# A decoder block on one Trainium2 core: larger portions for the attention, seven products for the first half of a gating projection, and a later read of the residual

## The chip, the cores and the metric

The kernel runs on one core of one Trainium2 chip. The metric is the device time of one execution in microseconds; lower is better. Three executions before the change took 1574.31, 1574.32 and 1574.69 us, a median of 1574.32. A further execution was recorded by the hardware profiler, and all durations and positions in this text come from it.

Engine names in the profile: PE is TensorE (matmuls), PEld its weight loads, DVE is VectorE, ACT is ScalarE, POOL is GpSimd, SP is the engine whose queue issues most DMAs. L12 is line 12 of the kernel before.

## The reference

One layer of a decoder trunk: 256 positions, 2048 channels, everything in float32. Three token mixers share one input projection, a gate per channel weighs each of them, and a feed-forward part follows.

```python
h = rms_norm(x, norm_mix_pre)
proj = h @ w_in                       # a_in, b_in, q, kv, nsa_g, merge_g
y_a = conformer_conv(a_in, ...)       # GLU, causal depthwise convolution of 31, LayerNorm, swish, @ w_a_out
y_b = chunked_spatial_gating(b_in, ...)                                   # ..., @ w_b_out
y_c = native_sparse_attention(q, kv, nsa_g, ...)   # compressed, selected and window attention, @ w_c_out
g_a, g_b, g_c = split(sigmoid(merge_g), 3)
mixed = (g_a * y_a + g_b * y_b + g_c * y_c) @ w_o
x = x + rms_norm(mixed, norm_mix_post)
h = rms_norm(x, norm_ffn_pre)
u_g, u_v = split(causal_dwconv3(h @ w_up), 2)
x = x + rms_norm((silu(u_g) * u_v) @ w_down, norm_ffn_post)
```

merge_g has 3 x 2048 columns: 2048 gates for each of the branches A (convolution), B (spatial gating) and C (attention).

## The kernel before

**Exact float32 from fp32r.** TensorE multiplies in a format called fp32r. Every operand is therefore split into a high part (the value rounded to fp32r, by ScalarE) and a low part (the remainder, by VectorE), and a product is three matmuls: high x high, high x low, low x high. `mm_t` (L195 to L198) issues such a triple; its three lines are the ones the profile shows for the projections with tokens on the partitions.

**Weights.** All weights stream from memory once. `fetch` (L104) reads 128 x 1024 float32 (512 KB) through SP's queue into one of five buffers `wraw`. `piece` (L132) and `weights` (L906) split it into `whi` and `wlo`, which have four buffers each; these eight buffers are a ring used in program order by everything that streams weights, and `ring` (L913) takes them for the sevens too. `granule` (L151) is two pieces, 24 matmuls in a gating projection.

**Scratch.** Three rings of large on-chip buffers matter here: `s16` with three buffers (xt, cv, At, Bt, Ct, ep, mh, ml, x2 in their turn) and one more outside P1 (mac, then y1, sf, back), `s8` with four, and `q1` with twelve buffers of 128 x 256. PSUM has four banks with the tag acc for the projections and four for everything else; `banks(2, 1)` recasts the second four as two single banks and one double one while the attention runs, and `banks(4, 0)` turns them back.

**Order of stages.** RMSNorm and the input projections come first, up to about 303 us in the profile. Then come the gated branches, `branch(bi, act_of)` (L994). Branch 0 is B, with its activations in Bt; branch 1 is A, with At; branch 2 is C, with Ct. For every column block of 512 output channels a branch runs the gating projection (four quarters of 24 matmuls, tiles pg, from hT), takes tanh of the gates (mg), runs the branch's own output projection (two halves of 24, tiles py), and adds the gated product into `mac`. Branches 0 and 1 have four column blocks. Branch 2 has two; the other half of its columns is done by seven products (below). After that come w_o (its first 1024 columns by seven products), the up-projection with the short convolution, and the down-projection in two halves of columns, `Pair(0)` and `Pair(1)`.

**Portions of background work.** Much of the work of the three mixers doesn't stream weights: the depthwise convolution (`conv_gen`), the layer norm of branch A with its activations At (`lna_gen`, L483), the compressed keys and values (`cmp_prep`, `cmp_gen`, L593 and L610), the scores of the compressed part (`cmp_attn`), and the attention itself (`attn`, L856). Each is a Python generator that issues a few instructions and yields a cost in nominal nanoseconds. The generators wait in a queue `bg`, and the projections call `pump` (L92) between their weight tiles:

```python
    def pump(ns):
        debt[0] = min(debt[0], 0.0) + ns if not bg else debt[0] + ns
        while bg and debt[0] > 0:
            try:
                debt[0] -= next(bg[0])
            except StopIteration:
                bg.popleft()
```

Each call adds one portion of `ns` units to an account and issues background work until the account is used up. The portion has a size for every stage; for the branches it is `BG`. In a branch one portion is issued after each 24 matmuls. `until(name)` (L200) issues all background work up to a mark, without an account: branch 0 needs "B" (Bt complete), branch 1 "A" (At), branch 2 "C" (the attention, Ct). `cmp_gen` streams weights too: its w1 pieces come through `piece`, in the same `wraw`, `whi` and `wlo` buffers, and its matmuls (zp) multiply them with bk, which `cmp_prep` writes. Program order sets who gets a buffer and which instruction has priority where several are ready; splits in `piece` are raised in priority by `PR`, 1000 places, and the framework orders each engine's instructions by these priorities and its own simulated times. Where the text speaks of `fixed` (L889) or `in_line` (L190), the order on an engine is written out by hand instead.

**Seven products.** `in_sevens` (L970) computes two column blocks at once, 2 x 128 tokens by 2 x 512 columns. For three pairs of k-tiles (`NG` = 3) it uses a scheme of seven block products where eight are usual: sums and differences of weight blocks, made by VectorE (`Seven.seven`, L940), meet sums and differences of activations (`sums4`, L837). Such a pair costs 21 matmuls in place of 24. The ten other k-tiles go the usual way. A `Seven` needs four banks for the results and four for side products, so all of the PSUM. The sums of hT for the gating projections are made in the background (`input_sums`, tile sh); those of the mixed activations, for w_o, are made after the gating stage by `sums4` into tiles `sm` (L1104 to L1107). `mix_gen` (L1047) transposes finished column blocks of mac into mh and ml.

**The residual.** The input of the last residual addition, y1, is written to memory (`spill`, L1345) and read back into `back` during the second half of the down-projection. That half runs through ten quads (`second.quad(j)`, one pair of k-tiles by seven products each) with plain k-tiles in between, and keeps six plain tiles (`kept`) for the end. After the loop, SP's queue gets a row of gains (L1508), `second.combine()` gathers the side products, and the six kept tiles finish the four results one after another, followed by the norm, the residual addition (`fin`, L1532) and the stores.

Of the kernel before, what the change touches and what calls it, by code (L numbers as in the profile page):

```python
# [30 lines left out]
D = 2048  # L32
T = 256
# [9 lines left out]
BA, BB, BC, BG = 2100, 2200, 2200, 2500  # L43
# [14 lines left out]
def block(ctx: ExitStack, tc: tile.TileContext, x, xf, fp, cst, rows, sgw, w1, w2, wf_a, wt_bv, wf_bu, wf_c,  # L58
# [935 lines left out]
    def branch(bi, act_of):  # L994

        for cb in range(2 if bi == 2 else 4):
# [46 lines left out]
            if bi == 2:  # L1043
                bg.append(mix_gen(cb))
            pump(BUDGET)

    def mix_gen(cb):  # L1047

        for j in range(2 * cb, 2 * cb + 2):
# [10 lines left out]
            if j < NG:  # L1060
# [8 lines left out]
    branch(2, lambda: Ct_box["t"])  # L1069
    mh, ml = mix["h"], mix["l"]  # L1070


    gates = s8([128, 2, 2, 512], F32, "gates")
    tt = s8([128, 2048], F32, "tt")
    pr = Seven([PS.tile([128, 512], F32, tag="acc", name=f"pga{i}") for i in range(4)],
               [bank([128, 512], f"pgb{i}") for i in range(4)])
    pr.at = lambda t, n: gates[:, t, n]
# [11 lines left out]
    def wp(n, k):  # L1089
        return weights(wt_p[20 + 2 * n + k // 4][:, k % 4 * 512:k % 4 * 512 + 1024])  # L1090

    pump(1e6)
# [4 lines left out]
    for n in range(2):  # L1097
        for t in range(2):
            fixed(V, V.tensor_add, gates[:, t, n], pr.c[t][n], gates[:, t, n])
            fixed(S, S.activation, gates[:, t, n], gates[:, t, n], AF.Tanh, scale=rh[:, t:t + 1])  # L1100
        if n == 0:
            early.append(wp(0, 4))
    with tc.issue_after(seq[V][0]):
        for j in range(NG):  # L1104
            if j % 2 == 0:
                mix[j // 2] = s8([128, 2, 2, 4, 128], R, f"sm{j}")
            sums4(*mix["a", j], mix[j // 2][:, j % 2], f"m{j}")  # L1107
    pump(1e6)
    Ct = Ct_box["t"]
    for n in range(2):  # L1110
        cb = 2 + n
        py = [bank([128, 512], f"pyc{t}") if n == 0 else PS.tile([128, 512], F32, tag="acc", name=f"pyd{t}")
              for t in range(2)]
        for k in range(8):
            if k % 2 == 0:
                hi, lo = early.pop(0) if early else wp(n, k)
# [540 lines left out]
```

## Time and profile before

| what | value |
|---|---|
| median of three executions | 1574.32 us |
| the profiled execution, its own time | 1575.5 us |
| its span on the core | 1573.8 us |
| TensorE busy | 1561.2 us, 99% of the span |
| VectorE busy | 1274.0 us, 81% |
| ScalarE busy | 906.6 us, 58% |
| DMA, mean over the span | 194 GB/s read and written |

The stages by the profile's clock: input projections and the layer norm's inputs to 303 us, branch 0 to 443, branch 1 to 608, the two column blocks of branch 2 to 688, the seven-product stage of its other half to 731 and its products to 753, w_o to 842, the up-projection to 1335, the down-projection's first half to 1448 and its second to 1564.6; the rest of the 1573.8 is the last norm, addition and store.

How to read it: all positions are microseconds from the start of the span. A row of a timeline has the start, the busy time, the engine, the line, the operation and its output and input tiles, a count where several equal ones are put together, and in brackets the engine's idle time before it and what ended that. A row of busy times by stretch has the stretch, its length, and then for each engine the busy time and the count of instructions in brackets, the granted TensorE clock (1.00 is full speed), the DMA engines' mean busy share and GB/s. TensorE's matmuls are pipelined: the listed duration of a 128x512 matmul is 0.39 us, but in a steady stream one begins every 0.227 us.

### The profile page before, as it was taken

The page shows a single profiled execution, that of the slowest core. Times are in us where ns is not written, and L with a number is a line of the kernel's source. Part 1 is how long each engine was busy: PE and PEld are TensorE (multiplying, and loading weights), DVE is VectorE, ACT ScalarE, POOL GpSimd, SP SyncE. Part 2 cuts the span into 40 slices and gives each one's busy share as a digit, 9 for nine tenths or more (in the row PEclk, how much of TensorE's full clock was granted, in tenths as well). Part 3 has the DMA queues.
Part 4 walks back from the last instruction along what each step waited for, and adds up shares of the span by engine and source line. Part 5 has one row for each costly group of instructions (what it writes and reads, how often), then busy time and mean ns, then how long its engine had stood idle before and what let it go on. Part 6 is the DMA issues. An engine that isn't in the chain of part 4 may idle for free.

```text
span 1573.8 us, 22431 instructions
## 1 busy us (share of the span) xinstructions
PE 1561.2 (99%) x8155; PEld 1324.4 (84%) x8155; DVE 1274.0 (81%) x2192; ACT 906.6 (58%) x1462; POOL 17.7 (1%) x46
## 2 busy tenths in 40 slices
PE   9999999999999999999999999999999999999997
PEld 7888889888888787788888888888888888888876
DVE  7799999858866655479878988888777777899898
ACT  7544544447646775656566655555555555556563
POOL 1000020000000000000000000000000000000000
PEclk9999999999999999999999999999999999999999
DMA  9565556665765445456784666666666666766672
GB/s 376 181 193 180 190 178 206 197 196 179 235 200 160 155 140 173 135 164 211 251 271 162 200 188 189 189 191 192 189 188 192 187 195 189 227 208 207 201 269 93
DMA packets 85440, 307.95 MB, mean 196 GB/s; under 512 B 9808, under 2 KB 10832, under 8 KB 84304
## 3 DMA queue, kind: packets, MB, share of 16 engines
q1 hardware_dynamic: 83952, 301.91, 60.1%
q0 software_dynamic: 944, 4.19, 0.7%
q8 instruction: 64, 1.05, 0.3%
q10 hardware_dynamic: 432, 0.41, 0.1%
q14 instruction: 48, 0.39, 0.1%
HBM read 301.23 MB, written 4.19 MB: 194 GB/s over the span
## 4 chain that ended last, share of the span: by engine, by line
PE 96%; DVE 2%; DMA 1%; ACT 0%; issue 0%; DVEq 0%; SPq 0%; ACTq 0%
PE ps L176 29%; PE ps L183 15%; PE pd0b L930 5%; PE pg L197 5%; PE pg L198 5%; PE pg L196 5%; PE pd1a L930 4%; PE py L197 2%; PE py L198 2%; PE py L196 2%; PE poa L930 2%; PE pga L930 2%; PE pd0a L930 2%; PE po L198 1%; PE po L196 1%; PE po L197 1%
## 5 line engine op out<-in xcount | busy, mean ns | idle before, releaser
L148 DVE TENSOR_TENSOR wlo<-wraw,whi 128x1024 fp32r<-128x1024 f32 x400 | 486.3, 1218 | 117.0 <-ACT whi L147 110.0
L147 ACT ACTIVATE whi<-wraw 128x1024 fp32r<-128x1024 f32 x400 | 418.8, 1052 | 186.7 <-PE pg L198 79.4
L176 PE MATMUL ps<-h2T,whi 128*128 128x512 f32 x1360 | 325.0, 391 | 0.0
L176 PEld LDWEIGHTS ps<-h2T,whi 128*128 128x128 f32 x1360 | 249.8, 188 | 48.2
L183 PEld LDWEIGHTS ps<-h2T,wlo 128*128 128x128 f32 x1360 | 174.5, 191 | 6.7
L183 PE MATMUL ps<-h2T,wlo 128*128 128x256 f32 x1360 | 176.6, 283 | 0.0
L176 PE MATMUL ps<-hT,whi 128*128 128x512 f32 x640 | 157.4, 392 | 0.0
L218 ACT ACTIVATE t<-ps 128x256 f32<-128x256 f32 x125 | 47.6, 382 | 187.1 <-PE ps L176 186.7
L176 PEld LDWEIGHTS ps<-hT,whi 128*128 128x128 f32 x640 | 116.0, 189 | 21.2
L198 PE MATMUL pg<-whi,hT 128*128 128x512 f32 x320 | 125.9, 393 | 0.0
L197 PE MATMUL pg<-wlo,hT 128*128 128x512 f32 x320 | 125.8, 393 | 0.0
L196 PE MATMUL pg<-whi,hT 128*128 128x512 f32 x320 | 122.2, 393 | 0.0
L895 DVE TENSOR_TENSOR wlowraw<-wraw,whiwraw 128x1024 fp32r<-128x1024 f32 x72 | 87.0, 1222 | 28.3 <-ACT whiwraw L895 27.1
L219 DVE TENSOR_TENSOR t<-ps,t 128x256 f32<-128x256 f32 x125 | 52.5, 421 | 70.4 <-ACT t L218 70.0
L479 DVE SCALAR_TENSOR_TENSOR cv<-hb,fps,cv 128x256 f32<-128x256 f32 x240 | 104.8, 476 | 0.2 <-ACT cv L475 0.2
L895 ACT ACTIVATE whiwraw<-wraw 128x1024 fp32r<-128x1024 f32 x72 | 75.3, 1058 | 33.6 <-PE pd0b L930 8.0
L183 PEld LDWEIGHTS ps<-hT,wlo 128*128 128x128 f32 x640 | 84.6, 190 | 4.7
L183 PE MATMUL ps<-hT,wlo 128*128 128x256 f32 x640 | 86.8, 283 | 0.0
L197 PEld LDWEIGHTS pg<-wlo,hT 128*128 128x128 f32 x320 | 60.1, 188 | 13.8 <-issue 1.1
L198 PEld LDWEIGHTS pg<-whi,hT 128*128 128x128 f32 x320 | 60.1, 188 | 12.7 <-issue 0.7
L196 PEld LDWEIGHTS pg<-whi,hT 128*128 128x128 f32 x320 | 59.8, 188 | 12.3 <-issue 0.3
L1385 ACT ACTIVATE fa<-fs,fps 128x256 f32<-128x256 f32 x88 | 52.4, 595 | 1.1 <-DVE fs L221 0.9
(1258 smaller groups left out, 2652.1 us busy)
## 6 DMA issues: line engine op xcount, KB each, us to landing
wraw<-in_wf_up_dram SPq DMA_DIRECT2D x176, 512.0 KB, 4.3
wraw<-in_wt_g_dram SPq DMA_DIRECT2D x80, 512.0 KB, 3.8
wraw<-in_wt_p_dram SPq DMA_DIRECT2D x48, 512.0 KB, 4.0
wraw<-in_wt_dn_dram SPq DMA_DIRECT2D x48, 512.0 KB, 4.4
wraw<-in_wf_a_dram SPq DMA_DIRECT2D x32, 512.0 KB, 4.5
wraw<-in_wt_dq_dram SPq DMA_DIRECT2D x20, 512.0 KB, 4.8
qa<-in_wt_dq_dram SPq DMA_DIRECT2D x20, 512.0 KB, 4.2
wraw<-in_wf_bu_dram SPq DMA_DIRECT2D x16, 512.0 KB, 4.2
```

The costliest lines, as they stand in the source:

```text
L147: S.activation(hi[:, :n], raw[:, :n], AF.Copy)
L148: V.tensor_sub(lo[:, :n], raw[:, :n], hi[:, :n].bitcast(F32))
L176: ins = PE.matmul(ps[:, :, ts], lhsT=ws[k // 8][0][:, c:c + 128], rhs=mov[:, k, :, ts], start=(k == 0 and not t), stop=(k == n - 1), skip_ ...
L183: ins = PE.matmul(ps[:, 1, ts], lhsT=ws[k // 8][1][:, c:c + 128], rhs=mov[:, k, 0, ts], start=False, stop=False, skip_group_check=True).ins
L196: PE.matmul(ps, lhsT=xh, rhs=hi, start=first, stop=False)
L197: PE.matmul(ps, lhsT=xh, rhs=lo, start=False, stop=False)
L198: return PE.matmul(ps, lhsT=xl, rhs=hi, start=False, stop=last).ins
L219: V.tensor_add(t1 if rb is not None else dst, ps[:, 0], t1)
L479: V.scalar_tensor_tensor(ca[:, j], hb[:, j, k:k + T], w(j, k), ca[:, j], op0=ALU.mult, op1=ALU.add)
L895: seq[eng] = [op(*args, **kw).ins]
L930: ins = PE.matmul(bank, lhsT=a[x], rhs=w[y], start=first and j == 0, stop=last and j == 2).ins
L1385: S.activation(a, s, AF.Identity, bias=fps[:, C_FB + f:C_FB + f + 1], scale=w[2])
```

## The change

There are three parts.

**The portions.** `BG`, the size of a portion in the branches, goes from 2500 to 5000 units.

**The first half of the third gating projection.** `branch(2, ...)` is gone. Both halves of branch C's columns now run through `in_sevens`, in a loop over `cp` = 0, 1: the gating projection of 1024 columns by seven products, then the two output projections (py20 and py21, py30 and py31) with their products added into mac. The weights for the gates of columns 4096 to 5119 are laid out as the existing seven-product weights are. Everything that is in the background must be done before the first of the two stages, so `until("C")` comes right behind branch 1; mh and ml are allocated there. The sums of the mixed activations are written into sh, the tile that held the sums of hT, in place of two tiles sm.

**The residual.** The read of `back` moves from behind the sixth quad of the second half (j == 5) to behind the last quad and the row of gains.

```diff
-BA, BB, BC, BG = 2100, 2200, 2200, 2500
+BA, BB, BC, BG = 2100, 2200, 2200, 5000
...
-        for cb in range(2 if bi == 2 else 4):
+        for cb in range(4):
...
-                    until("BAC"[bi])
-                    if bi == 2:
-                        mix["h"] = s16(P1, [128, KT, T], R, "mh")
-                        mix["l"] = s16(P1, [128, KT, T], R, "ml")
+                    until("BA"[bi])
...
-            if bi == 2:
-                bg.append(mix_gen(cb))
             pump(BUDGET)
...
-    branch(2, lambda: Ct_box["t"])
-    mh, ml = mix["h"], mix["l"]
...
+    until("C")
+    mh, ml = mix["h"], mix["l"] = [s16(P1, [128, KT, T], R, "m" + x) for x in "hl"]
+    Ct = Ct_box["t"]
...
-    in_sevens(pr, wt_gp, wt_gq, hx, acts_h, tt, "g")
-    early = [wp(0, k) for k in (0, 2)]
...
+    for cp in range(2):
+        gates = s8([128, 2, 2, 512], F32, f"gates{cp}")
+        if cp == 0:
+            tt = s8([128, 2048], F32, "tt")
+        pump(1e6)
+        pr = Seven([PS.tile([128, 512], F32, tag="acc", name=f"pg{cp}a{i}") for i in range(4)],
+                   [bank([128, 512], f"pg{cp}b{i}") for i in range(4)])
+        pr.at = lambda t, n: gates[:, t, n]
+        in_sevens(pr, wt_gp[cp], wt_gq[cp], hx, acts_h, tt, f"g{cp}")
+        early = [wp(2 * cp, k) for k in (0, 2)]
...
+        if cp:
+
+            with tc.issue_after(seq[V][0]):
+                for j in range(NG):
+                    sums4(*mix["a", j], sh[:, j], f"m{j}")
+        for n in range(2):
+            cb = 2 * cp + n
...
+            bg.append(mix_gen(cb))
+            pump(1e6)
...
-        if j == 5:
-            back = s16(P0, [128, 2, D], F32, "back")
-            for t in range(2):
-                nc.sync.dma_start(back[:, t], spill[:, t])
...
     nc.sync.dma_start(gain[:, 1024:2048], row(3072, 1024))
+    back = s16(P0, [128, 2, D], F32, "back")
+    for t in range(2):
+        nc.sync.dma_start(back[:, t], spill[:, t])
     second.combine()
```

More of the change, by code (lines that the diff above doesn't have):

```diff
@@ L1068, in block @@
     until("A")
-    branch(2, lambda: Ct_box["t"])
-    mh, ml = mix["h"], mix["l"]
[L1073 to L1077, printed above, removed]
+    until("C")
+    mh, ml = mix["h"], mix["l"] = [s16(P1, [128, KT, T], R, "m" + x) for x in "hl"]
+    Ct = Ct_box["t"]
     def parts(s, ks):
@@ L1087, in acts_h, with wp @@
         return s4, hx(2 * j + 1, H1), hx(2 * j, H1), s1, s3, s2, hx(2 * j + 1, H2)
-    def wp(n, k):
-        return weights(wt_p[20 + 2 * n + k // 4][:, k % 4 * 512:k % 4 * 512 + 1024])
-    pump(1e6)
+    def wp(cb, k):
+        return weights(wt_p[16 + 2 * cb + k // 4][:, k % 4 * 512:k % 4 * 512 + 1024])
     order_of(())
     seq[S] = [gated[0]]
-    in_sevens(pr, wt_gp, wt_gq, hx, acts_h, tt, "g")
-    early = [wp(0, k) for k in (0, 2)]
-    for n in range(2):
-        for t in range(2):
[L1099 to L1102, printed above, removed]
@@ L1508, in block @@
     nc.sync.dma_start(gain[:, 1024:2048], row(3072, 1024))
+    back = s16(P0, [128, 2, D], F32, "back")
+    for t in range(2):
+        nc.sync.dma_start(back[:, t], spill[:, t])
     second.combine()
```

49 lines of the change are left out of this document (21 added, 28 removed).

## The prediction

> **What bounds the kernel now.** I read the page first: the busy times and the chain of work that ended last.
>
> ```profile
> PE 1561.2 (99%) x8155; PEld 1324.4 (84%) x8155; DVE 1274.0 (81%) x2192; ACT 906.6 (58%) x1462; POOL 17.7 (1%) x46
> PE 96%; DVE 2%; DMA 1%; ACT 0%; issue 0%; DVEq 0%; SPq 0%; ACTq 0%
> ```
>
> TensorE is the bound nearly everywhere: the chain lies on it for 96% of the span. So an edit is worth the matmuls that it takes away, plus the places where TensorE waits, minus the new waits. A busy TensorE says little about waits, so next I read the spacing of matmuls from the chain in order of time, in the seven-product stage that exists already (tiles pga, pgb):
>
> ```profile
> 704.72 7.49 PE pga L930 x33
> ```
>
> 7.49 us for 33 is 0.227 us for a 128x512 matmul, in a stage of seven products as elsewhere (226 took 51 us in the first row below). Where TensorE falls short of that, it waits. The busy times by stretch (columns: length, then TensorE, weight load, VectorE, ScalarE as busy us and count, clock, DMA share, GB/s) show one such place, around the read of the residual:
>
> ```profile
> 1449.00:1500.00 51.00, 51.00 (x226) 42.24 (x225) 45.15 (x53) 32.07 (x38) 0.00 (x0) 1.00 0.62 197
> 1500.00:1521.00 21.00, 20.57 (x89) 16.10 (x87) 18.62 (x21) 12.39 (x13) 0.00 (x0) 1.00 0.85 318
> 1521.00:1548.00 27.00, 26.01 (x110) 20.40 (x111) 26.89 (x32) 17.20 (x19) 0.00 (x0) 1.00 0.49 149
> ```
>
> At 0.227 us the last two stretches, 48 us, hold 211 matmuls; there are 199, so about 2.8 us are lost. The timelines of SP, ScalarE, VectorE and TensorE say how:
>
> ```profile
> 1498.84 0.80 SPq L1499 DMA_DIRECT2D back<-spill  x2
> 1499.74 2.46 SPq L107 DMA_DIRECT2D wraw<-in_wt_dn_dram  x1
> 1510.03 1.06 ACT L895 ACTIVATE whiwraw<-wraw 128x1024 fp32r<-128x1024 f32 x1 [2.48 <-DMA wraw<-in_wt_dn_dram]
> 1511.12 1.22 DVE L895 TENSOR_TENSOR wlowraw<-wraw,whiwraw 128x1024 fp32r<-128x1024 f32 x1 [2.12 <-ACT whiwraw L895]
> 1521.29 0.50 PE L930 MATMUL pd1a<-wlowraw,gh 128*128 128x512 f32 x1 [0.62 <-DVE wlowraw L895]
> ```
>
> The two 1 MB reads go out ahead of the weight piece of 1499.74, which lands about 10 us later; VectorE, which splits weights with almost no gap here (26.89 us of 27), idles 2.12 us, and TensorE later runs into it.
>
> **The change part by part.** *Sevens for the first half.* Three pairs of k-tiles go from 24 matmuls to 21 each: 9 x 0.227 = 2.04 us less on TensorE, on the path. The weight fetches stay 16 of 512 KB on SP (10 plain, 6 of pairs). VectorE gets the sums of three quads:
>
> ```profile
> 688.00:732.00 44.00, 43.90 (x197) 35.90 (x196) 40.30 (x52) 25.22 (x30) 0.00 (x0) 1.00 0.65 207
> PEld pga L930 <- DVE wlowraw L895: 0.5, 1, 0.5
> ```
>
> In the stage that exists VectorE is busy 40.3 us of 44 and TensorE still 43.9, so the sums lie beside matmuls; if that cover went, they would show in full. What shows now is its start, 0.5 us in the list of waits at most. A second such start costs 0 to 0.5, I take 0.3. Writing the later sums into sh, allocating mh and ml earlier and the same count of product matmuls cost nothing: they lie off TensorE's path, and sh was last read before.
>
> *Residual behind the last quad.* The 2.12 us of VectorE idle goes, and with it as much of TensorE's 2.8, for VectorE has no other gap there; next late is VectorE's own pace, so some 0.7 stays. Gain 2.1 (bounds 1.5 and 2.8). On SP the reads now come behind every weight fetch and the row of gains, with nothing but the stores of the result after them. Their own waits are long over by then (the space of sf was last read by the fifth quad; the row of gains before them waits for the last quad's scratch). They must land before their first reader:
>
> ```profile
> back<-spill SPq DMA_DIRECT2D x2, 1024.0 KB, 8.4
> 1559.56 2.74 DVE L1532 SCALAR_TENSOR_TENSOR fin<-fin,rsyd,back 128x512 f32<-128x512 f32 x4
> ```
>
> Issued behind the gains (about 1546.5), 8.4 us later is 1555, 4.6 us ahead of that reader; both move with the stage. Hidden, cost 0; twice the landing time would show 4 us.
>
> *Portions twice as large.* This is the part that decides. The background work is issued by units of cost. When branch 0 begins about 18,800 units of the depthwise convolution are left (114,000 units so far against budgets of 95,200). Then come the layer norm of branch A (2,415 units to its first total on TensorE, lnpm; 5,175 to the second, lnpv; 3,400; 9,120 for eight tiles), cmp_prep (3,800) and cmp_gen, whose four w1 pieces cost 1,300 each. So lnpm stands at 21,200 units and the first w1 piece at 42,700. One portion is issued per 24 matmuls (5.44 us), from 303 us on. By 2,500: lnpm with the 9th portion, 303 + 9 x 5.44 = 352; the w1 piece with the 18th, 401. The trace has both there, for TensorE works near program order, while VectorE runs ahead of its portions where its inputs allow (the operand of lnpm is done at 329.9):
>
> ```profile
> 329.45 0.42 DVE L492 TENSOR_TENSOR lnm<-lnm,cv 128x256 f32<-128x256 f32 x1
> 351.66 0.43 PE lnpm L486 x2
> 365.27 0.42 DVE L504 TENSOR_TENSOR lnv<-lnv,lnsq 128x256 f32<-128x256 f32 x1
> 370.26 0.43 PE lnpv L486 x2
> 389.83 0.13 POOL L599 MEMSET bt<- 128x16 f32 x1 [163.66 <-DVE At L521]
> 391.52 1.53 ACT L1013 ACTIVATE mg<-pg,rh 128x256 f32<-128x256 f32 x4
> 394.69 1.06 ACT L147 ACTIVATE whi<-wraw 128x1024 fp32r<-128x1024 f32 x1
> 396.09 0.42 ACT L606 ACTIVATE bk<-bt 128x256 fp32r<-128x256 f32 x1
> 397.48 1.05 ACT L147 ACTIVATE whi<-wraw 128x1024 fp32r<-128x1024 f32 x1
> 399.92 0.75 DVE L607 TENSOR_TENSOR bk<-bt,bk 128x256 fp32r<-128x256 f32 x2
> 400.09 1.05 ACT L147 ACTIVATE whi<-wraw 128x1024 fp32r<-128x1024 f32 x1
> 401.38 0.28 PE L618 MATMUL zp<-whi,bk 128*128 128x256 f32 x1
> 401.58 2.01 ACT L147 ACTIVATE whi<-wraw 128x1024 fp32r<-128x1024 f32 x2
> 403.82 1.06 ACT L147 ACTIVATE whi<-wraw 128x1024 fp32r<-128x1024 f32 x1 [0.23 <-PE zp L618]
> ```
>
> By 5,000: lnpm with the 5th portion, 303 + 27.2 = 330.2, just behind its operand; the first two w1 pieces with the 9th, 352; the other two with the 10th, 357.5. The pieces move 49 us forward, the layer norm that stands before them only 21.5. And the matmuls zp need bk, which follows the layer norm's tiles: the scratch of cmp_prep (bt) waits for a buffer that At leaves (the POOL row). In the kernel before the first chunk of bk is ready at 400.3 (the first of the two at 399.92), 1.1 us ahead of its matmul, 48.7 us behind lnpm.
>
> Why TensorE would stop and not go on with the gates: w1 pieces and gate pieces share one ring of four split buffers, taken in program order. The split at 403.82 waits for a zp matmul: its buffer was that of the split four back, 397.48. So 397.48 and 394.69 are the first two w1 pieces, and they took their buffers before bk was done. In the changed kernel two buffers go to w1 pieces at 352; TensorE still gets the two gate pieces of that quarter (24 matmuls, to 357.5), then the other two w1 pieces hold the rest, and no piece of the product can be split until zp runs.
>
> How long? In the kernel before lnpv waited on TensorE from 365.7, when its operand was done, to 370.3, its place in the order; by larger portions that place is long past, so 4.6 us of the 48.7 go: bk at 330.4 + 44.1 = 374.5, a wait of 17.0 us. That is the upper end, since ScalarE, which carries the last stretch, loses the weight splits while TensorE stands:
>
> ```profile
> 378.00:402.00 24.00, 21.80 (x43) 1.00 0.58 184
> ```
>
> Of its 21.8 us here, one split of 1.05 per 12 matmuls (2.72 us) over 21.6 us makes 8.4, and the four tanh 1.5; without them 11.9 remain, 0.55 of it. 17.0 x 0.55 = 9.4; I take 9.5. The lower end: from lnpm to the operand of lnpv took 14.0 us for 23 small operations of about 0.4 us, with VectorE and ScalarE idle in between; done without gaps on two engines that is some 5 us, so all comes 9 us sooner, and 8 x 0.55 = 4.5 us of stand are left. The second half of bk (kv = 1) needs the first half's scratch, but product and gate pieces stand between: 0 to 2, taken as 0.
>
> After such a stand the clock has to be counted. Its rows, at the start and behind the last matmul (1564.18):
>
> ```profile
> 1.42 4.02 PE L288 MATMUL warm<-wz 128*128 128x512 bf16 x9 [1.42 <-POOL wz L285]
> 1565.00:1568.00 3.00, 0.00 (x0) 0.00 (x0) 2.69 (x12) 0.71 (x3) 0.00 (x0) 0.86 0.00 0
> 1568.00:1574.00 6.00, 0.00 (x0) 0.00 (x0) 2.44 (x5) 0.00 (x0) 0.00 (x0) 0.50 0.46 175
> ```
>
> 3 us behind the last matmul the granted clock is 0.50, and the first nine matmuls of the run take 4.02 us where nine at 0.227 take 2.04: a stand of 9 us ends in a start that loses 2.0 us (0 if weights are late then anyway; I take 2.0). The Trainium skill, "TensorE: Matmul & The Clock Gate", section "What's actually happening", puts this as a rule: after an idle window of about 3.4 us the array runs at half clock until it has been busy for about 3.4 us more. By that the restart loses 1.7 us and the sum would be 0.3 lower; the rows here agree on the half clock, and no stand inside the kernel shows it yet.
>
> The rest of larger portions: VectorE and ScalarE work comes earlier, beside matmuls; the attention's own matmuls are as many as before.
>
> Sum: -2.04 + 0.3 - 2.1 + 9.5 + 2.0 = +7.7 us. The profiled execution took 1575.5 (span 1573.8), 1.2 above the median 1574.32. So 1583.2 for that execution, 1582.0 against the median.
>
> **The rivals.** *No stand at the w1 pieces: faster.* Place: 357.5, the pieces' first matmul. If the first chunk of bk is there by then, or the gate pieces get the buffers first, only the rest of the sum counts: -2.04 + 0.3 - 2.1 = -3.8, 1570.5 us. For it: VectorE and ScalarE are half idle in branch 0,
>
> ```profile
> 303.00:335.00 32.00, 32.00 (x143) 26.51 (x142) 19.46 (x26) 14.46 (x17) 0.00 (x0) 1.00 0.64 201
> 335.00:357.00 22.00, 22.00 (x99) 18.22 (x98) 13.51 (x21) 9.20 (x11) 0.00 (x0) 1.00 0.56 177
> ```
>
> (VectorE 33 us of 54, ScalarE 24), so there is room to be early. Against it: the order of splits above, and lnpm cannot come before 330, which leaves 27 us for a chain that takes 48.7 now. The point where it decides: each us of stand beyond 3.8 makes the change a loss.
>
> *A short stand.* bk arrives 1 to 5 us after 357.5; with the clock the stand eats the gain: 1571.5 to 1577.5, most of it within 0.2% (3.1 us, about what a measurement of this kernel can tell from no change).
>
> *The attention is late as well.* Larger portions do not make it quicker if its own chain sets the pace:
>
> ```profile
> 494.36 0.28 DVE L781 CUSTOM_DVE_ANT_0 ep<-s,cs 128x128 f32<-128x128 f32 x1
> L752 PE MATMUL O<-ep,kkv x48: 592/592/644, 505.8 to 665.2; 128*64 128x512 f32 x48
> L196 PE MATMUL py<-whi,Bt x64: 387/389/397, 324.3 to 442.6; 128*128 128x512 f32 x64
> L198 PE MATMUL py<-whi,At x64: 388/389/501, 471.3 to 607.7; 128*128 128x512 f32 x64
> 608.00:666.00 58.00, 12.01 (x72) 6.97 (x72) 2.90 (x8) 20.96 (x60) 1.00 0.46 144
> ```
>
> Its second unit starts at 494.4 and the last values end at 665.8, 171 us. It needs the large buffer that Bt leaves with branch 0: 443, some 5 us of attention matmuls moved there, and the stand and its clock, 460. So it ends at 631. Branch 1 (608) ends after 11.5 us of stand and clock and at least the 12.0 us of TensorE that the attention's tile ep had behind 608 (the last row is that of ep alone), 632; the first new stage of sevens needs the attention's PSUM banks 48 matmuls (10.9 us) later, 643. A margin of 12 us: an attention 12% slower (20 us) costs 8 us, 1590.
>
> **How the numbers follow.** Stand of over 5 us: 0.53, 1582 its likeliest; with the attention late too 0.05, 1590; short stand 0.13; none 0.29, 1570.5. So faster 0.29, same 0.13, slower 0.58. The likeliest case alone runs from 1577 (5 us of stand, half the clock's loss) to 1590 (17.0, all of it). The range must reach the faster case: 1569.7 to 1590, leaving out the tail of a late attention and of a larger gain.
>
> **What would show it.** Stand: matmuls missing between 355 and 380, zp as the first behind the gap, the granted clock under 1 there. Sevens: tiles like pga twice, 18 matmuls fewer than plain for the two halves, 0.227 us apart. Residual: no 2.1 us idle of VectorE near 1500, under 1 us lost on TensorE there, and the reads landing before their reader. Attention: its last values before the first stage of sevens needs its banks. The forecast is wrong if bk comes much sooner behind lnpm than 44 us, or if gate and product pieces pass the w1 pieces in the ring.

## The result and the profile after

The changed kernel takes 1593.01 us (median of four, 1592.22 to 1593.84) where the kernel before takes 1574.51 on the same chip (1574.31 to 1574.92): a ratio of 1.0117, interval 1.0100 to 1.0135, 18.5 us slower. The forecast was 1582.0, in a range that ended at 1590.0. The sign came from the stand of TensorE that the forecast named; that stand lasted nearly twice the time taken for it.

Line numbers of the changed kernel are one lower than those before, up to the changed places. The busy times and the chain of the profile page after:

```profile
PE 1559.4 (98%) x8146; PEld 1323.1 (83%) x8146; DVE 1291.6 (81%) x2210; ACT 912.7 (57%) x1465; POOL 18.2 (1%) x46
PE 94%; DVE 3%; DMA 1%; ACT 1%; issue 1%; ACTq 0%; DVEq 0%
```

Nine matmuls fewer, as said. TensorE's busy time falls by 1.8 us, and the span grows by 17.7 (1591.5 against 1573.8; the medians differ by 18.5, because the profiled execution of before lay 1.0 us above its median and that of after 0.3): all of the loss is time in which TensorE does nothing or goes slowly. The list of waits names where (engine and line, what it waited for, us in total, times, the longest):

```profile
PE zp L617 <- DVE bk L606: 16.8, 1, 16.8
PE py L196 <- DVE wlo L147: 1.5, 1, 1.5
PE s L751 <- ACT pct L738: 1.2, 1, 1.2
```

The first row is the stand of the forecast: one wait of 16.8 us, of the first matmul on a w1 piece, for bk. TensorE's timeline has its place:

```profile
356.84 0.39 PE L197 MATMUL pg<-whi,hT 128*128 128x512 f32 x1
374.04 0.58 PE L617 MATMUL zp<-whi,bk 128*128 128x256 f32 x1 [16.81 <-DVE bk L606]
388.28 0.50 PE L196 MATMUL py<-wlo,Bt 128*128 128x512 f32 x1 [1.51 <-DVE wlo L147]
```

The last gate matmul before the stand starts at 356.84, where the forecast had the gates run out at 357.5, and behind it comes zp, not the next product. That the weights had nowhere to go is seen on ScalarE, which makes the splits, and on SP, which fetches:

```profile
354.59 1.06 ACT L146 ACTIVATE whi<-wraw 128x1024 fp32r<-128x1024 f32 x1
357.26 1.06 ACT L146 ACTIVATE whi<-wraw 128x1024 fp32r<-128x1024 f32 x1 [1.61 <-PE pg L197]
375.94 1.06 ACT L146 ACTIVATE whi<-wraw 128x1024 fp32r<-128x1024 f32 x1 [1.78 <-PE zp L617]
```

```profile
354.17 6.05 SPq L106 DMA_DIRECT2D wraw<-in_w_dram  x3
378.28 0.33 SPq L106 DMA_DIRECT2D wraw<-in_wt_p_dram  x1
```

ScalarE splits no weight from 358.3 to 375.9, and the split that ends this pause waits for a zp matmul: w1 pieces held the ring. No weight is fetched from 360.2 to 378.3 either: SP's longest wait between 350 and 400, 18.0 us, is for a split on VectorE (wlo), which reads the fetch buffer last. So the five fetch buffers behind the ring were full.

The wait of 1.51 us at 388.28 (and 0.36 just before) looks like one for a weight that was fetched too late, but it isn't. The piece in question is the one fetched at 378.28, and it landed 5.2 us later, at 383.4. Its rows on ScalarE and VectorE:

```profile
384.93 1.06 ACT L146 ACTIVATE whi<-wraw 128x1024 fp32r<-128x1024 f32 x1 [1.04 <-issue]
386.35 0.74 DVE L606 TENSOR_TENSOR bk<-bt,bk 128x256 fp32r<-128x256 f32 x2
387.02 1.21 DVE L147 TENSOR_TENSOR wlo<-wraw,whi 128x1024 fp32r<-128x1024 f32 x1
```

The view gives no releaser for the split at 384.93. By the semaphores in the trace it was held until 384.88, when the product matmul that ended at 384.84 gave its ring buffer free. The other three buffers then held w1 pieces again, those of the second half (kv = 1; the three `in_w` fetches of the row at 354.17), whose matmuls begin at 390.82. VectorE, which wrote the second half of bk between its splits and had no idle time from 379.65 to 388.69, then made the low part 1.0 us after the high part was ready. So this is the same effect once more, smaller: 1.9 us of waits.

The clock around the stand, in stretches (columns as in the prediction):

```profile
357.00:359.00 2.00, 0.22 (x1) 0.00 (x0) 1.93 (x5) 1.06 (x1) 0.00 (x0) 1.00 0.25 76
359.00:361.00 2.00, 0.00 (x0) 0.00 (x0) 2.00 (x5) 0.75 (x2) 0.00 (x0) 0.72 0.58 205
361.00:374.00 13.00, 0.00 (x0) 0.00 (x0) 10.44 (x38) 12.75 (x32) 0.50 (x4) 0.50 0.10 38
376.00:377.00 1.00, 1.00 (x7) 1.00 (x7) 0.00 (x0) 0.99 (x1) 0.00 (x0) 0.52 0.00 0
377.00:378.00 1.00, 1.00 (x10) 1.00 (x10) 0.97 (x1) 0.59 (x1) 0.00 (x0) 1.00 0.00 0
```

Two things are to be seen. Half clock holds from about 360 to 377, so from 374 to 377 TensorE works 2.9 us at half speed and loses 1.4 (13 matmuls that take 1.56 us at 0.12 each). And in the 13 us from 361 to 374 ScalarE is busy 12.75 and VectorE 10.44: the layer norm went on at the pace of ScalarE, with no weight split beside it.

The second part, the sevens (windows of the two stages, tiles pg0a and pg1a):

```profile
642.00:686.00 44.00, 44.00 (x195) 36.39 (x194) 37.51 (x48) 23.57 (x25) 0.00 (x0) 1.00 0.59 192
706.00:751.00 45.00, 45.00 (x203) 37.20 (x202) 38.97 (x48) 26.10 (x33) 0.00 (x0) 1.00 0.56 182
```

TensorE is busy without a break in both, and neither tile stands in its list of waits. The attention, in the groups of its first and its last matmuls:

```profile
L751 PE MATMUL s<-kkv,qf x128: 272/374/480, 437.7 to 588.5; 64*128 64x128 f32 x64, 64*128 64x256 f32 x64
L751 PE MATMUL O<-ep,kkv x48: 592/592/643, 462.8 to 627.5; 128*64 128x512 f32 x48
```

It is done at 628.1, 14 us before the first stage of sevens begins (642.9) and 27 before that stage needs the attention's banks (its first pg0b matmul, 655.2). It took 190 us from its first scores.

The third part, the read of the residual, in the same two views as before (stretches, and SP's timeline):

```profile
1517.00:1539.00 22.00, 21.40 (x96) 17.27 (x94) 20.15 (x23) 13.45 (x14) 0.00 (x0) 1.00 0.90 328
1539.00:1566.00 27.00, 26.30 (x112) 20.61 (x113) 26.90 (x31) 17.29 (x19) 0.00 (x0) 1.00 0.47 148
```

```profile
1517.06 0.33 SPq L1501 DMA_DIRECT2D back<-spill  x1
1517.48 0.38 SPq L106 DMA_DIRECT2D wraw<-in_wt_dn_dram  x1
1517.91 0.42 SPq L1501 DMA_DIRECT2D back<-spill  x1
```

The read did not move behind the last quad. It goes out at 1517.06, 18.2 us later than the 1498.84 of before, and the whole kernel is 18.2 us later by then (the first matmul on pd1a starts at 1466.5 for 1448.3). The program's new place only put one weight piece between the two reads.

### Where the 17.7 us come from

For a sum over all of TensorE I take every gap from the start of one matmul to the start of the next, minus the usual gap for that shape (0.227 us for 128x512, 0.120 for 128x256), and add these up over a stretch. It holds waits, half clock and the small steps between unlike matmuls alike; the entries depend by up to 0.3 us on what is taken as usual for the few smaller shapes. Medians are those of each kernel's own runs, taken in several rounds in which the kernel before had medians from 1573.3 to 1574.8; the ratios further below are always to the kernel before of the same round. The kernels of the lower rows are told of below.

| kernel | 340 to 420 | 420 to 440 | 600 to 680 | 1480 to the end | median, us |
|---|---|---|---|---|---|
| before | 0.5 | 0.1 | 2.3 | 3.1 | 1574.5 |
| changed | 21.0 | 1.8 | 0.8 | 2.5 | 1593.0 |
| portions_alone | 21.2 | 1.7 | 0.7 | 3.1 | 1595.0 |
| small_portions | 0.5 | 0.1 | 18.7 | 1.1 | 1588.1 |
| staged | 0.5 | 0.1 | 18.7 | 2.4 | 1588.0 |
| staged_held | 0.5 | 0.1 | 18.8 | 1.0 | 1588.4 |
| bk_first | 20.0 | 1.8 | 0.8 | 2.2 | 1592.1 |
| bk_first_spread | 15.9 | 0.5 | 0.9 | 1.1 | 1585.9 |
| w1_middle | 14.2 | 0.5 | 0.8 | 2.0 | 1584.8 |
| w1_later | 3.7 | 0.0 | 0.8 | 1.1 | 1573.3 |
| w1_later_held | 3.7 | 0.0 | 0.8 | 1.1 | 1573.4 |
| portions_paced | 3.7 | 0.0 | 0.8 | 3.0 | 1576.3 |
| read_held | 0.5 | 0.1 | 2.3 | 1.0 | 1573.1 |
| read_moved | 0.5 | 0.1 | 2.3 | 1.1 | 1572.9 |

For the changed kernel: +20.5 in 340 to 420 (17.0 of stand, 1.4 behind it with the half clock, 2.3 at 385 to 388 from the second half of bk, against 0.5 before), +1.7 in 420 to 440 (the attention's first scores are queued behind a short chain, the third row of the waits), -2.0 for nine matmuls, -0.6 at the residual, and the rest (-1.9) mostly in 600 to 680 (-1.5, the attention's end and the start of the sevens) and at the very start of the run (-0.8). That makes the 17.7.

### The profile page after: what moved, and what is told of

It is laid out like the page before. It is cut to its first block, busy times and chain, and to the rows that moved or that the text cites. A ratio compares the mean times of both kernels' runs of the same rounds, so it can differ in the third digit from the quotient of the medians.

```text
span 1591.5 us, 22436 instructions
## 1 busy us (share of the span) xinstructions
PE 1559.4 (98%) x8146; PEld 1323.1 (83%) x8146; DVE 1291.6 (81%) x2210; ACT 912.7 (57%) x1465; POOL 18.2 (1%) x46
## 4 chain that ended last, share of the span: by engine, by line
PE 94%; DVE 3%; DMA 1%; ACT 1%; issue 1%; ACTq 0%; DVEq 0%
PE ps L175 29%; PE ps L182 15%; PE pd0b L929 5%; PE pg L195 4%; PE pg L197 4%; PE pg L196 4%; PE pd1a L929 3%; PE py L196 3%; PE py L197 3%; PE py L195 3%; PE poa L929 2%; PE pg1a L929 2%; PE pg0a L929 2%; PE pd0a L929 2%; PE po L195 1%; PE po L197 1%
## 5 line engine op out<-in xcount | busy, mean ns | idle before, releaser
L147 DVE TENSOR_TENSOR wlo<-wraw,whi 128x1024 fp32r<-128x1024 f32 (+1 forms) x376 | 457.4, 1218 | 108.4 <-ACT whi L146 102.0
L146 ACT ACTIVATE whi<-wraw 128x1024 fp32r<-128x1024 f32 (+1 forms) x376 | 393.3, 1052 | 156.4 <-PE pg L197 58.4
L894 DVE TENSOR_TENSOR wlowraw<-wraw,whiwraw 128x1024 fp32r<-128x1024 f32 x90 | 108.6, 1223 | 37.6 <-ACT whiwraw L894 36.1
L894 ACT ACTIVATE whiwraw<-wraw 128x1024 fp32r<-128x1024 f32 x90 | 94.6, 1057 | 48.6 <-PE py L197 17.4
L196 PE MATMUL pg<-wlo,hT 128*128 128x512 f32 x256 | 100.7, 394 | 0.0
L197 PE MATMUL pg<-whi,hT 128*128 128x512 f32 x256 | 100.7, 393 | 0.0
L195 PE MATMUL pg<-whi,hT 128*128 128x512 f32 x256 | 98.6, 393 | 0.0
L196 PEld LDWEIGHTS pg<-wlo,hT 128*128 128x128 f32 x256 | 48.1, 188 | 10.8 <-issue 1.1
L197 PEld LDWEIGHTS pg<-whi,hT 128*128 128x128 f32 x256 | 48.1, 188 | 10.5 <-issue 0.7
L195 PEld LDWEIGHTS pg<-whi,hT 128*128 128x128 f32 x256 | 47.9, 188 | 10.4 <-issue 0.7
```

The lines of the kernel that those rows point to most:

```text
L146: S.activation(hi[:, :n], raw[:, :n], AF.Copy)
L147: V.tensor_sub(lo[:, :n], raw[:, :n], hi[:, :n].bitcast(F32))
L195: PE.matmul(ps, lhsT=xh, rhs=hi, start=first, stop=False)
L196: PE.matmul(ps, lhsT=xh, rhs=lo, start=False, stop=False)
L197: return PE.matmul(ps, lhsT=xl, rhs=hi, start=False, stop=last).ins
L894: seq[eng] = [op(*args, **kw).ins]
```

## The experiments

The theory: portions of 5,000 bring the w1 pieces into the split ring before bk is written; everything that streams weights then waits for bk. Its rivals: the loss comes from the missing branch 2; or from portions of that size as such, whatever their order; or from the number of w1 pieces that come at once.

### One part alone, and one part undone

*portions_alone*: the kernel before, with nothing but the portions changed.

```diff
-BA, BB, BC, BG = 2100, 2200, 2200, 2500
+BA, BB, BC, BG = 2100, 2200, 2200, 5000
```

> The kernel before with only the portions changed, 2500 to 5000 units. Theory (w1 pieces take the split buffers ahead of bk): TensorE stands 15 to 18 us ahead of the first zp matmul, near 357 us, and 3 to 5 us more go with the clock and late weights behind it; branch 2 is still there, so nothing is won elsewhere: 1592 to 1597 us. Rival (the loss comes from the missing branch 2, with the attention uncovered): no stand there, 1573 to 1577 us.

Measured: 1594.97 us, ratio 1.0135 (1.0121 to 1.0149). Its list of waits begins as that of the changed kernel does:

```profile
PE zp L618 <- DVE bk L607: 16.8, 1, 16.8
```

The loss comes with the portions alone (20.2 us here); with portions of this size the missing branch 2 has no part in it.

*small_portions*: the changed kernel with portions of 2,500.

```diff
-BA, BB, BC, BG = 2100, 2200, 2200, 5000
+BA, BB, BC, BG = 2100, 2200, 2200, 2500
```

> The changed kernel with portions of 2500 again. Theory: no stand at zp, bk 1 us ahead of its matmul as before; but the attention starts near 486 us as before and takes 170 to 190 us more, while branch 1 ends near 621 us, so the first stage of sevens waits for its end with TensorE nearly idle: 25 to 45 us lost there, 1595 to 1615 us. Rival (the larger portions were not needed): 1570 to 1574 us.

Measured: 1588.08 us, ratio 1.0092 (1.0077 to 1.0107). The stand is gone (0.5 us in 340 to 420) and another loss has come, in the first stage of sevens, which begins its plain k-tiles at 607.5 and needs the attention's banks for its side products. The stretches of this kernel:

```profile
608.00:620.00 12.00, 12.00 (x63) 10.11 (x62) 3.78 (x12) 10.58 (x30) 0.00 (x0) 1.00 0.22 73
620.00:650.00 30.00, 18.04 (x81) 9.77 (x80) 12.57 (x31) 16.27 (x39) 0.57 (x1) 0.83 0.17 52
650.00:660.00 10.00, 10.00 (x44) 8.24 (x45) 7.30 (x9) 4.88 (x5) 0.00 (x0) 1.00 0.56 179
```

From 620 to 650 TensorE is busy 18 us of 30, at a mean clock of 0.83, while the attention's last units go through ScalarE and VectorE with few matmuls left to cover them. The place was expected, the price (18.7 us) is below the 25 to 45 written: with its last part uncovered the attention takes 167 us from its first scores (481.6 to 648.5), where it takes 184 in the kernel before and 190 in the changed one. So without branch 2 the attention has to start sooner than at 482 us, and the small portions cost about as much at the end as the large ones do at the start.

### Larger portions only later

*staged*: the changed kernel with 2,500 units in branch 0 and 5,000 in branch 1; *staged_held* also holds the read of the residual on SP behind the last weight fetch (by the line marked "read_held only" further below).

```diff
+    BUDGET = 2500
     branch(0, lambda: Bt_box["t"])
+    BUDGET = BG
     branch(1, lambda: At)
```

> The changed kernel with portions of 2500 in branch 0 and 5000 in branch 1, so that layer norm and w1 pieces keep their old pace and only the attention gets larger portions. Theory: no stand at zp; the attention starts near 455 us in place of 486, needs 150 to 170 us more and is done by about 617 to 632, when the first stage of sevens needs its banks: 1571 to 1574 us. Rival (the attention needs the larger portions from the start): a gap of 5 us or more ahead of the first stage of sevens, 1576 us or more.

> As staged, with the reads of back also held on SP behind the last weight fetch. Theory: 1.5 us under staged, 1569.5 to 1572.5 us, since the loss near 1520 to 1545 is another one than the stand. Rival: no difference from staged (under 0.5 us).

Measured: staged 1587.95 us (1.0090, 1.0076 to 1.0104) and staged_held 1588.43 (1.0094, 1.0079 to 1.0108). Both forecasts missed. The first scores of the compressed part and of the attention in staged:

```profile
L709 PE MATMUL sc<-kcb,qf x32: 194/276/277, 451.2 to 466.9; 128*128 128x32 f32 x32
L751 PE MATMUL s<-kkv,qf x128: 272/374/481, 481.7 to 626.1; 64*128 64x128 f32 x64, 64*128 64x256 f32 x64
```

The attention starts at 481.7, as with small portions, and not at 455: the compressed part ahead of it takes 30.5 us (451.2 to 481.7), as much as in the kernel before with its 2,500 (451.5 to 482.0). Where branch 0 had portions of 5,000 too it took 26.4 (changed kernel, 411.3 to 437.7) and 31.9 (w1_later, 415.5 to 447.4). So portions of 5,000 do little or nothing for the length of this chain of small steps; they decide when it begins. In the profiles the held read brings 1.3 us (2.4 to 1.0 in the last column), in the runs nothing.

### The order of bk and its weights

*w1_later*: one number. Each of the layer norm's eight At tiles is counted as 4,000 units in place of 1,140, so that less work fits a portion there and the w1 pieces come 22,900 units, 4.6 portions, later. All else in the program is the changed kernel.

```diff
-            yield 1140
+            yield 4000
```

> The changed kernel with the layer norm's eight At tiles at 4000 units each in place of 1140, which puts the w1 pieces some 25 us later (near 379 us in place of 352) and leaves portions at 5000 elsewhere. Theory of the order: bk is ready when its first piece is split, the stand at zp shrinks from 17.0 us to under 3. Theory of the density: four pieces a portion still cost 3 to 10 us in waits for weights. Both: 1576 to 1584 us. If only the order counts: 1572 to 1575. Rival (stand is due to portion size whatever the place): a stand over 8 us stays, 1585 us or more.

Measured: 1573.26 us, 0.9994 of the kernel before (0.9985 to 1.0004), and 19.7 us less than the changed kernel. The wait for bk in its list of waits, and the end of its attention:

```profile
PE zp L617 <- DVE bk L606: 0.3, 1, 0.3
L751 PE MATMUL O<-ep,kkv x48: 592/592/643, 471.5 to 633.9; 128*64 128x512 f32 x48
```

16.8 us have become 0.3, and with them went the half clock and the waits of the second half. The attention, which starts at 447.4, ends at 634.5 beside the first stage of sevens (from 620.9) and holds nothing up. The stand came from the order of bk and its weights; the number of w1 pieces per portion, unchanged here, costs at most the 3.2 us by which 340 to 420 still stands above the kernel before, so by the time the case in which both count was wrong and the case in which only the order counts held. But this edit does two things at once: fewer of the layer norm's tiles now fit a portion as well, so the splits go between them. It doesn't show that a right order alone would be enough; bk_first below tests that.

*w1_middle*: the same with 2,500 units, to see whether the stand follows the distance.

```diff
-            yield 1140
+            yield 2500
```

> The changed kernel with the At tiles at 2500 units, between 1140 and 4000: the first w1 piece comes at (42,700 + 10,880) / 5000, the 11th portion, near 363, in place of 352. Theory: bk is ready near 374 to 376 whatever the portions, the ring runs dry some 5 us behind 363, so the stand at zp is 5 to 9 us and the half clock costs up to 2 more: 1579 to 1584 us. Rival (the stand ends in one step somewhere between the places): under 2 us of stand, 1572 to 1575, or all of it, over 1590.

Measured: 1584.82 us, ratio 1.0072 (1.0058 to 1.0086). TensorE's timeline at the stand:

```profile
368.91 0.39 PE L197 MATMUL py<-whi,Bt 128*128 128x512 f32 x1
379.42 0.58 PE L617 MATMUL zp<-whi,bk 128*128 128x256 f32 x1 [10.12 <-DVE bk L606]
```

The ring runs dry at 369 as expected; bk comes at 379, 3 to 5 us later than written, so the stand and the time are a little over what was expected (ScalarE still splits weights beside the layer norm until 371.6 here). Pieces at 352, 363 and 379: 16.8, 10.1 and 0.3 us of stand. It is a difference of two arrival times, not a step.

*bk_first*: cmp_prep goes ahead of the layer norm in the queue of background work, so that bk is early instead of its weights late.

```diff
-    bg.append(lna_gen())
+    lna = lna_gen()
+    bg.append(lna)
...
-        bg.append(cmp_prep(kv))
+        bg.insert(bg.index(lna), cmp_prep(kv))
         bg.append(cmp_gen(kv))
```

> The changed kernel with cmp_prep put ahead of the layer norm in the queue of background work, so that bk is written long before its w1 pieces come; portions stay at 5000. Theory: the stand of 17.0 us, the half clock behind it (1.4) and the late weights (2.4) go: 1570 to 1574 us, zp without a wait of over 1 us. Rival (portions of that size overload ScalarE and VectorE in branch 0 whatever the order): a gap of 8 us or more stays at zp or at the first product, 1583 us or more.

Measured: 1592.13 us, ratio 1.0115 (1.0101 to 1.0129). The wait for bk is gone from the list of waits, and others stand in its place:

```profile
PE py L195 <- ACT whi L146: 7.0, 3, 4.5
PE hp L629 <- ACT zs L625: 2.2, 1, 2.2
PE py L196 <- DVE wlo L147: 2.1, 2, 1.6
```

Nearly as much is lost between 356 and 396, in waits for splits and for small chains, as by the one stand. The granted clock is halved twice on the way (378.3 to 385.1 and 388.5 to 395.3); by the gaps of the matmuls in these stretches (0.43 us for 0.227) that is some 5 us of the 20, an estimate. The longest wait, 4.5 us, ends with a split that stands on ScalarE behind 5.2 us of the layer norm (from 373.63 to 378.85). So bk's place in the queue is not enough. The rival, that portions of this size overload ScalarE and VectorE whatever the order, held in its number, and no run refutes it: w1_later has the same portions and no such loss, but fewer tiles of the layer norm in each.

*bk_first_spread*: as bk_first (its edit isn't repeated), and the w1 pieces at 2,600 units, two per portion as before the change.

```diff
-            yield 1300
+            yield 2600
         zs = [q1(f"zs{kv}{a}") for a in range(2)]
```

> The changed kernel with cmp_prep ahead of the layer norm, as in bk_first, and the w1 pieces at 2600 units each in place of 1300: two per portion, as in the kernel before, in place of four. With bk early the stand at zp went, but 20 us of waits for weights and small chains were spread over 340 to 400. Theory (eight w1 pieces of 512 KB with only 8 short matmuls each come too densely for the queue, the splits and the layer norm beside them): 5 to 14 us less than bk_first, 1578 to 1587 us. Rival (the layer norm's own work beside the gates is what stalls it): within 3 us of bk_first, 1589 to 1595.

Measured: 1585.93 us, ratio 1.0081 (1.0067 to 1.0096), 6 us under bk_first: thinner pieces help. Most of what remains is one wait, shown on TensorE and on ScalarE:

```profile
384.00 0.79 PE L195 MATMUL pg<-whi,hT 128*128 128x512 f32 x1 [10.82 <-ACT mg L1013]
```

```profile
374.17 0.58 ACT L515 ACTIVATE lz<-cv,fps 128x256 f32<-128x256 f32 x1
383.13 1.53 ACT L1013 ACTIVATE mg<-pg,rh 128x256 f32<-128x256 f32 x4
```

The gates' tanh (mg), which empties the banks for the next block, stands in ScalarE's queue behind 9 us of layer norm. Whether its scratch buffers or the framework's priorities put it there wasn't settled. In w1_later, where the layer norm is issued more slowly, TensorE waits 1.0 us for the same tanh.

### The residual's read, and what the sevens are worth

*read_moved*: the kernel before with the read moved in the program as in the change. *read_held*: the same, and held on SP behind the last weight fetch. (One diff for both; the removed lines behind j == 5 are left out.)

```diff
     nc.sync.dma_start(gain[:, 1024:2048], row(3072, 1024))
+    back = s16(P0, [128, 2, D], F32, "back")
+    with tc.issue_after(fetched[0]):          # read_held only
+        for t in range(2):
+            nc.sync.dma_start(back[:, t], spill[:, t])
```

> The kernel before with the read of back moved in the program alone, as the change has it, and held by nothing. The traces have it in the middle of the quads on SP before and after the change alike. Theory (the move does nothing or very little, at most 0.5 us): 1574.0 to 1574.8 us. Rival (it is worth the 2.1 us of the forecast): 1572.0 to 1573.0 us.

> The kernel before with the read of back moved behind the last quad and held there on SP behind the last weight fetch (in the changed kernel it still goes out in the middle of the quads). Theory: the weight piece that took 10.2 us to land comes in time, the 2.1 us idle of VectorE near 1510 goes, and TensorE loses about 1 us in place of 3.1: 1571.7 to 1573.0 us. Rival 1 (VectorE's pace sets that stretch anyway): under 0.6 us won, 1573.9 to 1574.6. Rival 2 (the reads land too late for the last additions): above 1575 us.

Measured: read_moved 1572.94 us (0.9997, 0.9988 to 1.0006), read_held 1573.10 (0.9991, 0.9982 to 1.0000). To read these: the kernel before has two groups of times of its own, 1572.4 to 1573.5 and 1574.0 to 1575.2 (16 and 11 of the 27 runs beside read_moved), while all 22 runs of the two variants lie at 1572.3 to 1573.9. The stretches of read_moved, to be set beside 89 and 110 matmuls of the kernel before:

```profile
1500.00:1521.00 21.00, 21.00 (x95) 17.37 (x94) 20.59 (x24) 13.57 (x14) 0.00 (x0) 1.00 0.95 347
1521.00:1548.00 27.00, 26.50 (x116) 21.21 (x115) 26.86 (x31) 16.22 (x18) 0.00 (x0) 1.00 0.40 131
```

Twelve more matmuls pass in the same 48 us, and the loss from 1480 to the end falls from 3.1 us to 1.1. SP sends the reads at 1498 still, a weight piece between them:

```profile
1498.03 0.33 SPq L1507 DMA_DIRECT2D back<-spill  x1
1498.45 0.38 SPq L107 DMA_DIRECT2D wraw<-in_wt_dn_dram  x1
1498.88 0.42 SPq L1507 DMA_DIRECT2D back<-spill  x1
```

So the move in the program did not move the reads away, but one weight piece passed between them, and in that profile the loss went with it; holding both reads to the end (1533.91 in read_held) brought no more. It isn't reliable, since the changed kernel has the same order and lost 2.5 us. The time of read_moved lies in the range of the rival that it is worth 2.1 us, but that doesn't decide for the rival: the kernel before ran at a median of 1573.27 beside it, and the interval of the ratio holds 1. In the medians the move is worth nothing to 2 us, by which group the kernel before falls into; that these groups are the late and the timely weight piece is likely, but a profile of the lower group of the kernel before was not taken.

*portions_paced*: the kernel before, with portions of 5,000 and At tiles at 4,000 units. *w1_later_held*: w1_later, with the read held.

> The kernel before with portions of 5000 and At tiles at 4000 units; branch 2 and the early read stay. Against w1_later it isolates the sevens of the first half: 9 matmuls of 0.227 us, 2.04, and the 0.5 us with which the one stage of before started: 1575.3 to 1576.3 us. Rival (the second stage of sevens gains nothing, its sums or its start cost what the matmuls save): 1573 to 1574 us.

> As w1_later (At tiles at 4000 units), with the reads of back held on SP behind the last weight fetch as well. By read_held, where TensorE's loss in that stretch fell from 3.1 to 1.1 us: 0.0 to 0.7 us under w1_later, whose own loss there is only 1.1 us: 1572.5 to 1573.5. Rival (the two add up in full, as 1.7 us did in read_held): 1571.0 to 1572.0.

Measured: portions_paced 1576.28 us (1.0019, 1.0010 to 1.0028), w1_later_held 1573.36 (0.9998, 0.9989 to 1.0007). They ran side by side, and differ by the second stage of sevens and by the read: 2.9 us. Nine matmuls are 2.04 of it; the other 0.9 is the start of the stages and the read, not told apart. Holding the read added nothing to w1_later, whose last stretch was at 1.1 us already. The best versions, w1_later and w1_later_held, don't beat the kernel before by anything that these runs can tell: the sevens' 2 to 3 us are spent on the 3.2 us that branch 0 still loses with larger portions.

## Why the prediction was wrong in size and right in sign

*The place and the cause of the stand* held to the letter: the ring runs dry within 1 us of 357.5, zp is the first matmul behind the gap, w1 pieces hold the split buffers, bk ends it. portions_alone, w1_middle and w1_later show that most of the loss comes from it.

*Its length* is the step that failed: 9.5 us taken, 17.0 measured. The rows of the chain after (TensorE, VectorE):

```profile
333.71 0.60 PE L485 MATMUL lnpm<-lnm,ones 128*128 128x256 f32 x2
345.49 0.88 DVE L503 TENSOR_TENSOR lnv<-lnv,lnsq 128x256 f32<-128x256 f32 x2
350.72 0.60 PE L485 MATMUL lnpv<-lnv,ones 128*128 128x256 f32 x2
359.77 2.76 DVE L514 TENSOR_TENSOR cv<-cv,rsya 128x256 f32<-128x256 f32 x8
373.55 0.43 DVE L606 TENSOR_TENSOR bk<-bt,bk 128x256 fp32r<-128x256 f32 x1
```

The forecast had lnpm at 330.2, just behind its operand, and it came at 333.7: 3.5 us. It took 4.6 us off because lnpv's place in the order would be long past; but lnpv still starts 4.4 us behind its operand (346.3 to 350.7), almost as before the change. In both cases TensorE works on gates and products meanwhile, so the small matmul waits for its place on TensorE and not for its operand. That the framework's own simulated times put it there is likely, but not shown. The third part, that ScalarE goes faster without the splits, was about right: from the scaling of cv to bk 14.2 us (359.8 to 374.0) where it took 22.2 (378.1 to 400.3), 8.0 us less for the 7.5 taken. 3.5 and 4.4 are the 7.5 us by which the stand was too short, nearly.

That 17.0 is also the forecast's upper end is luck. That end had bk at 374.5 with no speed-up of ScalarE at all and with the 4.6 us gone; bk came at 374.0 with the speed-up, and with the two small matmuls late.

*The clock* cost 1.4 us for 2.0. The Trainium skill's rule ("TensorE: Matmul & The Clock Gate", "What's actually happening", half clock until some 3.4 us of work) gave 1.7; the trace has half clock for 2.9 us behind the stand, nearer to the rule than to the start of the run, from which the 2.0 was taken. Behind the stand of w1_middle half clock held for 4.9 us and cost 2.3, so the runs don't decide between the two.

*The second half of bk* was put at 0 to 2 us and taken as 0. It cost 1.9 us of waits (2.3 with the small steps around them). The forecast had set it aside because product and gate pieces stand between; they do, but w1 pieces of the second half held three of the four split buffers all the same. *Late weights*, the forecast's alternative to the clock's loss, weren't the cause, though no fetch had gone out for 18 us. This 2.3, the 1.7 at 436 that no term had, and the 1.5 of the residual that were not won are what carried the result past the range; the clock and the small gains (-1.9) took some of it back.

*Sevens*: 2.04 us, right; the start of the second stage was put at +0.3, and both stages together start with less than the one of before did.

*The residual*: the gain of 2.1 us was wrong in its mechanism. That the read goes behind every weight fetch was taken from the program's order, and SP's order is the framework's. The changed kernel won 0.6 us of the 2.1 in its profile.

*The attention* as a rival: its end was put at 631 and the margin at 12 us; it ended at 628, and the banks were needed at 655. That the end came so near is luck too. The forecast started it at 460, when branch 0 would leave the buffer of Bt; but its second unit writes ep from 448.4, while products still read Bt until 481:

```profile
L197 PE MATMUL py<-whi,Bt x64: 387/389/504, 324.0 to 480.9; 128*128 128x512 f32 x64
```

So it didn't wait for that buffer, and it took 180 us from there instead of 171. What it costs when it is late is what small_portions and staged show, 18.7 us.

## What to carry to other kernels

Where several streams share one ring of buffers in program order, a stream whose buffers are taken before its other operand is written stops all the others: before work is moved forward, compare its place with the time at which everything else that it needs is ready, and move the pace of that chain too (here one number, 1140 to 4000, was worth 19.7 us: it moved the weights behind bk and thinned out the layer norm beside the splits). A larger budget for background work only moves its starts; a chain that was paced by its own latencies (26 to 32 us of compressed scores, 167 to 190 of attention) stays about as long. And a DMA's place in the source is not its place on the queue where a framework orders the queues: look at the queue's timeline before a gain is booked on it.

## What the runs showed of the hardware

In the changed kernel the granted clock fell 2.7 us after TensorE's last matmul had ended (357.2; the mean of 0.72 over 359 to 361 puts the fall at 359.9) and rose 2.9 us after the first matmul of the restart (374.0 to 377.0). Neither time is a constant: in w1_middle the fall came 4.8 us behind the last matmul (369.3 to 374.1) and the rise 4.9 us behind the first (379.4 to 384.3). And in bk_first the clock was halved twice, though TensorE was never idle for more than 4.5 us at once. At half clock matmuls of 128x256 began every 0.21 us in place of 0.12, and those of 128x512 every 0.43 in place of 0.227. A stand also empties the fetch queue: no weight was fetched for 18 us. The next piece had landed all the same before its ring buffer came free.
